# Weight sums on GpSimd, one pool, loads in program order and stage borders by tiles in a decoder trunk in split fp32

## The chip, the cores and the metric

The kernel runs on one core of one Trainium2 chip. The metric is the device time of an execution in microseconds; below it is the median of the timed runs.

## The reference

One layer of a decoder trunk on x of 1024 tokens by 1024 channels, in fp32:

```
h  = rmsnorm(x);  z = h @ W_in               # 36 column blocks of 128
yA = conformer: GLU -> causal conv of 31 taps -> LayerNorm -> silu -> @ W_a
yB = short conv: B * conv3(C * V) -> @ W_b
x1 = x + (sigmoid(gA) * yA + sigmoid(gB) * yB) @ W_o
f  = gelu(conv3(rmsnorm(x1) @ W_up gate)) * (rmsnorm(x1) @ W_up value)   # 2816 channels
x2 = x1 + f @ W_down
x3 = x2 + sigmoid(rmsnorm(x2) @ W_pg) * (p @ W_p)
out = rmsnorm(x3)
```

## The kernel before

Channels lie on the 128 partitions and the 1024 tokens along the free axis, so a 128x1024 tile holds one block of channels. Each fp32 operand is kept as a high half, which a ScalarE cast makes (`hi`), and a low half, which VectorE makes by subtracting (`lo`); a block of a product is three matmuls of 128x512, hi by hi, hi by lo and lo by hi (`halve`, `split`, `mm`). Weights arrive as fp32 and are split on the chip too: `whi` and `wlo` for a whole block of 128x1024 (names `wr_hi`, `wr_lo` for those kept).

The stages, in order:

1. The start: the embedding product, the norm, and the first four input products as whole blocks.
2. The in stage: W_in in 16 pairs of column blocks, each by a Strassen scheme of seven products (`Pair.step(m)`, m from 1 to 7) in place of eight. A product m has 12 matmuls, a pair 84. `block_order` interleaves a pair with the next. Weight operands are quarters of a pair or one of four sums of quarters (s12 and s34, in `operand`), activation operands likewise (`right_sums`). The convs of 31 taps run in the background on VectorE (`bg`, `pump`); their results go to memory in `acc_d`, the short conv's in `s_d`, the gates in `gate_d`.
3. The b stage (four steps jj of two products by `half_products`, one w_b block a step), with the LayerNorm's mean and variance formed between its steps; the a stage (the same with w_a), which ends in the merged m; the o stage (eight products by w_o), which gives x1 and the activation operands of the up stage.
4. The up stage: 22 pairs of W_up by the same scheme; f goes to `f_d`.
5. The down stage in three chunks of 8, 8 and 6 blocks of f (`DCHUNKS`), then the tail: the embedding gate's eight products by w_pg over three stretches of tokens (`SEGS`, class `Item`), the final norm and the output. The tail's ScalarE and VectorE code is in the order written.

`Loader` issues weight loads and splits. `get(ahead=2)` returns the operand of the next product after it has split those up to two whole blocks further on (three in the tail), which is how far the casts stand ahead of the products that use them. PE runs in program order; on other engines a scheduler at build time fixes an order, and each engine then takes its instructions in that order. Loads stand on SP's queue.

## Time and profile before

| | |
|---|---|
| median of 3 timed runs | 1421.42 us (1421.0 to 1421.55) |
| the profiled execution, whole | 1422.73 us |
| its span in the profile | 1420.7 us |
| TensorE, busy in the span | 94% |
| VectorE, ScalarE, GpSimd, busy | 71%, 38%, 0% |
| mean granted TensorE clock | 0.97 of full |

The profiled execution is 1.31 us longer than the median, and its span 2.03 us shorter than itself. TensorE is the engine that is busy nearly throughout, so a stage is read by where TensorE waits in it and for whom.

### The profile page before, as it was taken

Reading aid. Unit: us, or ns where it says so; the run is one execution under the profiler, and the core shown is the slowest. Engines: PE = TensorE matmul, PEld = TensorE weight load, DVE = VectorE, ACT = ScalarE, POOL = GpSimd, SP = SyncE. Lnnn points to the kernel's source line nnn. Section 1 sums busy time; section 2 is a strip of 40 time slices with the busy share of each in tenths; the row PEclk is TensorE's granted clock in tenths of the full one; section 3 lists DMA queues with packets and bytes.
Section 4 is the critical chain, followed back from the end, with each engine's and each line's share of the span. In section 5 each row is a group of like instructions: output and inputs, shape, how many; then the busy total and the mean of one; then the engine's idle time right before and its main releaser. Section 6 shows DMA issues by size and latency. Waiting matters only on the chain.

```text
span 1420.7 us, 15176 instructions
## 1 busy us (share of the span) xinstructions
PE 1336.7 (94%) x5926; PEld 1101.5 (78%) x5926; DVE 1003.8 (71%) x1290; ACT 542.7 (38%) x788; POOL 1.2 (0%) x9
## 2 busy tenths in 40 slices
PE   9799999899989599979999999999978999999996
PEld 7678687678867488868888888888856888888896
DVE  6789999999834874678777777777764332145777
ACT  7342342233441523454444344344433221023554
POOL 0000000000000000000000000000000000000000
PEclk9899999999998799989999999999998999999998
DMA  9111231122455233422222222222255431111232
GB/s 358 61 30 45 81 127 60 45 104 92 160 175 195 89 121 117 141 82 74 90 89 89 68 81 83 81 89 90 90 175 220 153 119 37 45 52 54 88 93 93
DMA packets 46727, 146.88 MB, mean 103 GB/s; under 512 B 5184, under 2 KB 11584, under 8 KB 46656
## 3 DMA queue, kind: packets, MB, share of 16 engines
q1 hardware_dynamic: 46656, 145.92, 29.4%
q8 instruction: 46, 0.75, 0.2%
q14 instruction: 25, 0.20, 0.0%
HBM read 109.20 MB, written 36.70 MB: 103 GB/s over the span
## 4 chain that ended last, share of the span: by engine, by line
PE 73%; DVE 17%; DMA 5%; ACT 3%; issue 2%; SPq 0%; DVEq 0%; ACTq 0%
PE ps L569 39%; PE ps L158 33%; DVE acc L649 7%; DVE wb L136 2%; DMA x<-xT 2%; DMA x_d<-x 1%; DVE x L875 1%; DMA f<-f_d 1%; DVE sc_cv L649 1%; DVE lrstd L328 0%; DVE s L204 0%; DMA gate<-gate_d 0%; DMA x_raw<-xT 0%; DMA p_raw<-pT 0%; DMA s<-s_d 0%
## 5 line engine op out<-in xcount | busy, mean ns | idle before, releaser
L649 DVE SCALAR_TENSOR_TENSOR acc<-a,prm,acc 128x1023 f32<-128x1023 f32 (+14 forms) x120 | 155.0, 1291 | 0.0
L135 ACT CAST wb<-s 128x512 fp32r<-128x512 f32 x152 | 90.3, 618 | 114.3 <-DVE s L213 64.6
L158 PE MATMUL ps<-f_hi,whi 128*128 128x512 f32 x352 | 109.2, 392 | 16.3 <-ACT f_hi L135 16.3
L569 PE MATMUL ps<-xgs_hi,wb 128*128 128x512 f32 x352 | 116.4, 391 | 5.2 <-ACT xgs_hi L135 5.2
L957 DVE TENSOR_TENSOR x<-ps,x 128x512 f32<-128x512 f32 x46 | 29.6, 686 | 128.8 <-PE ps L158 128.8
L135 ACT CAST whi<-raw 128x1024 fp32r<-128x1024 f32 (+2 forms) x46 | 45.7, 996 | 194.8 <-PE ps L158 175.3
L569 PE MATMUL ps<-xgt_hi,wb 128*128 128x512 f32 x352 | 116.9, 393 | 0.7 <-ACT u L595 0.7
L569 PE MATMUL ps<-xg_hi,wb 128*128 128x512 f32 x352 | 115.6, 390 | 0.0
L136 DVE TENSOR_TENSOR wb<-s,wb 128x512 fp32r<-128x512 f32 x152 | 103.6, 695 | 10.0 <-ACT wb L135 9.9
L158 PE MATMUL ps<-f_lo,whi 128*128 128x512 f32 x352 | 109.3, 392 | 0.0
L158 PE MATMUL ps<-f_hi,wlo 128*128 128x512 f32 x352 | 108.9, 391 | 0.0
L569 PE MATMUL ps<-hss_hi,wb 128*128 128x512 f32 x256 | 88.7, 408 | 12.7 <-ACT wb L135 6.2
L158 PEld LDWEIGHTS ps<-f_hi,whi 128*128 128x128 f32 x352 | 66.5, 189 | 30.3 <-ACT f_hi L135 16.7
L569 PE MATMUL ps<-h_hi,wb 128*128 128x512 f32 x256 | 85.4, 395 | 2.2 <-DVE s L596 2.2
L569 PE MATMUL ps<-hst_hi,wb 128*128 128x512 f32 x256 | 84.4, 391 | 0.9 <-ACT u L595 0.7
L136 DVE TENSOR_TENSOR wb<-raw,wb 128x512 fp32r<-128x512 f32 x114 | 79.0, 694 | 6.6 <-ACT wb L135 6.6
L569 PEld LDWEIGHTS ps<-xgs_hi,wb 128*128 128x128 f32 x352 | 66.4, 189 | 19.1 <-ACT xgs_hi L135 5.6
L569 PEld LDWEIGHTS ps<-xgt_hi,wb 128*128 128x128 f32 x352 | 66.9, 190 | 15.1 <-ACT u L595 1.1
L158 PEld LDWEIGHTS ps<-f_lo,whi 128*128 128x128 f32 x352 | 66.2, 189 | 14.7 <-DVE f_lo L136 1.1
L158 PEld LDWEIGHTS ps<-f_hi,wlo 128*128 128x128 f32 x352 | 66.4, 189 | 13.8
L569 PEld LDWEIGHTS ps<-xg_hi,wb 128*128 128x128 f32 x352 | 66.1, 188 | 13.6
L569 PEld LDWEIGHTS ps<-hss_hi,wb 128*128 128x128 f32 x256 | 48.9, 194 | 29.5 <-DVE wb L136 9.5
(226 smaller groups left out, 2850.7 us busy)
## 6 DMA issues: line engine op xcount, KB each, us to landing
raw<-w_up SPq DMA_DIRECT2D x44, 512.0 KB, 3.4
raw<-w_in SPq DMA_DIRECT2D x36, 512.0 KB, 3.6
f_d<-v_t SPq DMA_DIRECT2D x22, 512.0 KB, 3.0
f<-f_d SPq DMA_DIRECT2D x22, 512.0 KB, 6.7
gate_d<-gate SPq DMA_DIRECT2D x16, 512.0 KB, 2.7
gate<-gate_d SPq DMA_DIRECT2D x16, 512.0 KB, 5.9
raw<-w_dn SPq DMA_DIRECT2D x16, 512.0 KB, 3.6
x_raw<-xT SPq DMA_DIRECT2D x16, 256.0 KB, 6.3
```

What stands on the lines that cost most here:

```text
L135: nc.scalar.copy(hi, src)
L136: nc.vector.tensor_sub(lo, src, f32(hi))
L158: nc.tensor.matmul(ps[:, :step], wt[:, b], xt[:, t : t + step], start=f, stop=l)
L569: nc.tensor.matmul(ps, wt[:, b], xt, start=f, stop=l, skip_group_check=True)
L649: nc.vector.scalar_tensor_tensor(dst[:, s:], src[:, : T - s], w(k), dst[:, s:], ALU.mult, ALU.add)
L875: nc.vector.tensor_add(r[:, c], ps, r[:, c])
L957: nc.vector.tensor_add(x1[j][:, c], ps, x1[j][:, c])
```

## The change

The four weight sums of a pair are made by GpSimd in place, in tiles that are loaded a second time for it; a pair's loads grow from 1 MB to 2 MB. Signs are turned so that only additions are needed; some sigmoids, conv taps (`neg_b`, `neg_f`) and two of the activation sums carry the sign, and the products of a pair are taken in another order. Of a pair's weight splits, seven of 128x512, three of 128x1024 and one of 128x512 remain.

The three pools become one of 51 slots. `Loader` sorts its loads by a distance ahead, counted in matmul passes of 512 columns (`AHEAD`), and SP's queue runs in program order too. Splits have a distance of their own, `SPLIT = 40` passes, where a whole block of 128x1024 counts 6 * 8 = 48 passes.

At the borders of stages, work goes by tiles: the s tiles are loaded and split within the last steps of the in stage, the gates of the b stage ahead of it, the LayerNorm's mean and variance are formed after steps jj = 0 and jj = 1, m is split by halves, the o stage runs by halves of the tokens with its norm by halves, six f tiles are loaded and split within the last steps of the up stage, and the first four products of the down stage start on two f tiles. The w_up loads are held until the o stage is nearly over.

```diff
-NRAW, NW, NBIG = 4, 6, 41
+NBIG = 51
+AHEAD = {"whole": 100, "r": 110, "q": 100, "s": 150}
+SPLIT = 40
...
     class Loader:
...
+        def add(self, src, nb, cuts=(), again=False):
+            key = ("whole", len(self.uses))
+            n = len(self.uses)
+            self.loads.append((n, "whole", key, (src, cuts, nb)))
+            self.splits.append((n, key, (cuts, nb)))
+            self.use(key, None, 6 * nb)
...
-                st = slot("s12")
-                WADD[0](nc).tensor_add(st[:, :q], a21, a22)
-                WADD[1](nc).tensor_sub(st[:, q:], st[:, :q], a11)
...
-                st = slot("s34")
-                WADD[2](nc).tensor_sub(st[:, :q], a11, a21)
-                WADD[3](nc).tensor_sub(st[:, q:], a12, s12[:, q:])
...
+            if kind == "r":
+                t = slot("raw_r")
+                nc.sync.dma_start(t, w1)
+            elif kind == "q":
+                t = slot("raw_q")
+                nc.sync.dma_start(t[:, :q], w2[:, q:])
+            else:
+                t, v = slot("s12"), slot("s34")
+                s1, s2, s3, s4 = t[:, :q], t[:, q:], v[:, :q], v[:, q:]
+                nc.sync.dma_start(s1, w2[:, :q])
+                nc.sync.dma_start(s2, w1[:, :q])
+                nc.sync.dma_start(v, w1)
+                a22 = slot("raw_a22")
+                nc.sync.dma_start(a22[:, :q], w2[:, q:])
+                for dst, src in ((s3, s1), (s1, a22[:, :q]), (s2, s1), (s4, s2)):
+                    nc.gpsimd.tensor_add(dst, dst, src)
...
-        def get(self, ahead=2):
+        def get(self, load=True):
+            i = self.at
             self.at += 1
-            i = self.at - 1
-            n, left = i + 1, ahead * 2
-            while left > 0 and n < len(self.specs):
-                left -= 1 if self.specs[n][0] == "block" else 2
-                n += 1
-            self.split(n)
+            now = self.cost[i]
+            while load and self.loaded < len(self.loads):
+                n, kind, key, _ = self.loads[self.loaded]
+                if n > i and (key[0] in self.held or self.cost[n] - now > AHEAD[kind]):
+                    break
+                self.fetch(self.loaded + 1)
+            while self.pending and (
+                self.pending[0][0] <= i or load and self.cost[self.pending[0][0]] - now <= SPLIT
+            ):
+                self.split(*self.pending.pop(0)[1:])
...
-    with tc.manual_schedule(engines={PE}):
+    with tc.manual_schedule(engines={PE, SP}):
...
-            TADD(nc).tensor_sub(t24[:, H0], xb[:, H1], t13[:, H0])
-            TADD(nc).tensor_sub(t24[:, H1], xb[:, H0], t24[:, H0])
+            nc.vector.scalar_tensor_tensor(t24[:, H0], t13[:, H0], -1.0, b1, ALU.mult, ALU.subtract)
+            nc.vector.scalar_tensor_tensor(t24[:, H1], t24[:, H0], -1.0, b0, ALU.mult, ALU.subtract)
...
+            left = len(in_order) - 1 - n
+            for at, c in ((8, 0), (7, 1), (2, 2), (1, 3)):
+                if left == at:
+                    s_t.append(load_split(s_d[c], "s"))
...
-        s_t = [split(load(s_d[c], "s"), "s") for c in range(KC)]
...
-            if jj == 2:
-                ssq = Ssq()
+            if jj == 0:
                 pm = [bank(), bank()]
...
-        inverse(lr)
+            if jj == 1:
+                for c in HALVES:
+                    ps = bank()
+                    cs_mm(ps, ones_c, cs, c)
+                    sqrt(lr[:, c], ps)
+                    inverse(lr[:, c])
...
-                m_t[j] = split(g, "m")
+                for c in HALVES:
+                    m_t[j, c.start] = half_split(g[:, c], "m")
...
+        def o_add(i, q, c):
+            j = i + 4 * q
+            r, h = xs[i, c.start], HALVES[q]
+            if q == 0:
+                xg[i, c.start] = slot("xg")
+            nc.vector.tensor_add(r[:, h], obank[j, c.start], r[:, h])
+            nc.scalar.activation(xg[i, c.start][:, h], r[:, h], AF.Copy, scale=col("g_ffn", j))
+            nc.sync.dma_start(x1_d[j][:, c], r[:, h])
...
+            left = len(up_order) - 1 - n
+            if left in (8, 7, 2, 1):
+                for _ in range(1 if left > 2 else 2):
+                    f_t.append(load_split(f_d[len(f_t)], "f"))
...
+                    ws = [ld.get() for _ in range(4)]
+                    pss = [[bank(), bank()] for _ in range(4)]
+                    for ks in (range(2), range(2, n)):
...
-            wpg = [ld.get(2), ld.get(1)]
+            wpg = [ld.get(), ld.get()]
...
-                    wpg.append(ld.get(3))
+                    wpg.append(ld.get())
```


ScalarE at the border of the b and a stages and through the a stage. `m_hi` and `m` are casts of the merged tile `gate`, two tiles a step; a step's products use one `whi`. Before, where the four steps of the a stage use whi_3177, 3272, 3372 and 3448 in turn, and the o stage 3524, 3600 and on:

```order
L135 CAST m_hi_3431<-gate_3366 128x1024
L135 CAST whi_3448<-raw_3370 128x1024
L135 CAST m_hi_3438<-gate_3368 128x1024
L135 CAST whi_3524<-raw_3446 128x1024
L135 CAST m_hi_3507<-gate_3442 128x1024
L135 CAST m_hi_3514<-gate_3444 128x1024
L135 CAST whi_3600<-raw_3522 128x1024
L135 CAST m_hi_3583<-gate_3518 128x1024
L135 CAST m_hi_3590<-gate_3520 128x1024
L135 CAST whi_3672<-raw_3598 128x1024
L135 CAST m_hi_3659<-gate_3594 128x1024
L135 CAST m_hi_3666<-gate_3596 128x1024
```

Of the change, where the steps use whi_3356, 3432, 3508 and 3584 in turn:

```order
L130 CAST m_3415<-gate_3214 128x512
L130 CAST m_3418<-gate_3214 128x512
L130 CAST m_3424<-gate_3216 128x512
L130 CAST m_3427<-gate_3216 128x512
L130 CAST whi_3432<-raw_3292 128x1024
L130 CAST m_3491<-gate_3218 128x512
L130 CAST m_3494<-gate_3218 128x512
L130 CAST m_3500<-gate_3220 128x512
L130 CAST m_3503<-gate_3220 128x512
L130 CAST whi_3508<-raw_3354 128x1024
```

The place on PE in the changed kernel where the step on whi_3356 ends and the next begins:

```order
L153 MATMUL ps_3386<-an_lo_3211,whi_3356 128x512
L153 MATMUL ps_3387<-an_lo_3211,whi_3356 128x512
L153 MATMUL ps_3386<-an_hi_3210,wlo_3357 128x512
L153 MATMUL ps_3387<-an_hi_3210,wlo_3357 128x512
L153 MATMUL ps_3436<-an_hi_3192,whi_3432 128x512
L153 MATMUL ps_3437<-an_hi_3192,whi_3432 128x512
```

Before, the cast of the last step's whi_3448 stood right behind the first tile of the first step (gate_3366), two steps early. Now the cast of the second step's whi_3432 stands behind the second tile of the first step (gate_3216), whose product is the one just ahead of it on PE; and so at each step after.

ScalarE over the LayerNorm. `acc` holds the conv results, `cs_hi` feeds the sums over channels, the `acc<-acc` rows are the silu. Before, where the first `whi` is that of the third step of the a stage, and the last that of the fourth:

```order
L135 CAST whi<-raw 128x1024
L325 ACT_TABLE_LOAD
L325 ACTIVATE lrstd<-ps,eps_t 128x512 x2
L839 ACT_TABLE_LOAD
L839 ACTIVATE acc<-acc,prm 128x1024 x2
L135 CAST an_hi<-acc 128x1024
L839 ACTIVATE acc<-acc,prm 128x1024
L135 CAST an_hi<-acc 128x1024
L839 ACTIVATE acc<-acc,prm 128x1024
L135 CAST an_hi<-acc 128x1024 x2
L135 CAST m_hi<-gate 128x1024
L135 CAST whi<-raw 128x1024
```

Of the change, where the first single `whi` is that of the b stage's step jj = 1, and the first of the three at the end that of step jj = 2:

```order
L130 CAST cs_hi<-ssq 128x1024
L130 CAST whi<-raw 128x1024
L362 ACT_TABLE_LOAD
L362 ACTIVATE lrstd<-ps,eps_t 128x512 x2
L890 ACT_TABLE_LOAD
L890 ACTIVATE acc<-acc,prm 128x1024 x2
L130 CAST an_hi<-acc 128x1024
L890 ACTIVATE acc<-acc,prm 128x1024
L130 CAST an_hi<-acc 128x1024
L890 ACTIVATE acc<-acc,prm 128x1024
L130 CAST an_hi<-acc 128x1024 x2
L130 CAST whi<-raw 128x1024 x3
```

Before, every w_b cast, and three of w_a, stood ahead of the silu. Now the cast for b step jj = 1 stands behind the squares and the cast of their sum, and the one for jj = 2 behind the whole silu and its four casts.

ScalarE in the tail, first stretch of tokens. `last<-last` is the gate's sigmoid of a product, `x1<-x1` scales the result, `last<-x1` and `fs<-x1` are squares, `whi` the next product's weights. Before:

```order
L1014 ACTIVATE x1_7301<-x1_7301,prm_69 128x448
L1008 ACTIVATE last_8831<-x1_7303 128x448
L135 CAST whi_8951<-raw_8902 128x1024
L135 CAST whi_8957<-raw_8949 128x1024
L995 ACTIVATE last_8961<-last_8961 128x448
L1014 ACTIVATE x1_7303<-x1_7303,prm_69 128x448
L1008 ACTIVATE last_8916<-x1_7305 128x448
L135 CAST whi_8995<-raw_8955 128x1024
L995 ACTIVATE last_8999<-last_8999 128x448
L1014 ACTIVATE x1_7305<-x1_7305,prm_69 128x448
```

Of the change:

```order
L1138 ACTIVATE fs_8920<-x1_7359 128x448
L1127 ACTIVATE last_8922<-last_8922 128x448
L1146 ACTIVATE x1_7359<-x1_7359,prm_63 128x448
L1140 ACTIVATE last_8843<-x1_7361 128x448
L130 CAST whi_8957<-raw_8835 128x1024
L1127 ACTIVATE last_8961<-last_8961 128x448
L1146 ACTIVATE x1_7361<-x1_7361,prm_63 128x448
L1140 ACTIVATE last_8922<-x1_7363 128x448
L130 CAST whi_8997<-raw_8908 128x1024
```

Before, the casts for the sixth and seventh product (whi_8951, whi_8957) stood ahead of the fourth product's sigmoid (last_8961). Now the cast for the fourth product (whi_8957) stands behind the third product's sigmoid (last_8922) and the square behind it; and so for each up to the eighth.

## Rows read from the trace of the kernel before

**Rows 1.** The page, busy time of each engine (share of the span) and instructions

```profile
PE 1336.7 (94%) x5926; PEld 1101.5 (78%) x5926; DVE 1003.8 (71%) x1290; ACT 542.7 (38%) x788; POOL 1.2 (0%) x9
```

**Rows 2.** Windows: busy us (instructions) of PE, PEld, DVE, ACT, POOL; PEclk; DMA share; GB/s

```profile
140.00:320.00 180.00, 167.61 (x703) 132.00 (x702) 180.00 (x218) 56.97 (x101) 0.00 (x0) 0.98 0.24 83
400.00:440.00 40.00, 34.11 (x128) 25.48 (x127) 13.40 (x15) 12.91 (x16) 0.00 (x0) 0.87 0.71 263
460.00:500.00 40.00, 24.01 (x94) 18.47 (x92) 32.64 (x32) 19.54 (x19) 0.00 (x0) 0.79 0.21 79
488.00:494.00 6.00, 3.42 (x7) 2.31 (x8) 4.98 (x5) 6.00 (x7) 0.00 (x0) 0.50 0.00 0
620.00:660.00 40.00, 31.92 (x128) 25.01 (x127) 31.14 (x36) 19.42 (x27) 0.00 (x0) 0.87 0.20 66
636.00:642.00 6.00, 4.69 (x10) 3.41 (x11) 5.88 (x8) 3.63 (x5) 0.00 (x0) 0.50 0.00 0
700.00:1000.00 300.00, 300.00 (x1325) 248.59 (x1325) 223.39 (x315) 123.51 (x189) 0.00 (x0) 1.00 0.24 83
1040.00:1080.00 40.00, 23.03 (x92) 17.62 (x92) 21.99 (x24) 13.78 (x14) 0.00 (x0) 0.79 0.80 298
```

**Rows 3.** Waits of PE: engine and line waited for, total us, times, longest

```profile
PE ps L158 <- ACT f_hi L135: 16.3, 1, 16.3
PE ps L158 <- ACT an_hi L135: 15.2, 1, 15.2
...
PE ps L569 <- ACT xgs_hi L135: 5.2, 1, 5.2
```

**Rows 4.** The chain that ended last in order of time: start us, us, what

```profile
128.45 1.18 DVE acc L649
...
302.45 0.73 DVE wb L136
...
422.04 5.31 DMA s<-s_d
427.37 1.05 ACT s_hi L135
...
478.42 6.46 DVE lrstd L328
```

**Rows 5.** Groups of VectorE by form: xcount, busy us, mean ns, idle before

```profile
L136 DVE TENSOR_TENSOR wb<-s,wb 128x512 fp32r<-128x512 f32 x152 | 103.6, 695 | 10.0 <-ACT wb L135 9.9
...
L136 DVE TENSOR_TENSOR wlo<-raw,whi 128x1024 fp32r<-128x1024 f32 x36 | 43.8, 1219 | 13.0 <-PE ps L569 8.4 <-ACT whi L135 4.6
...
L204 DVE TENSOR_TENSOR s<-raw 128x512 f32<-128x512 f32 x38 | 26.4, 696 | 0.0
...
L850 DVE TENSOR_TENSOR gate<-ps,gate 128x512 f32<-128x512 f32 x16 | 10.3, 686 | 7.8 <-PE ps L158 5.8 <-DMA gate<-gate_d 1.9
...
L851 DVE TENSOR_TENSOR gate<-gate 128x1024 f32<-128x1024 f32 x8 | 9.8, 1222 | 0.1
...
L328 DVE RECIPROCAL rstd<-rstd 128x512 f32<-128x512 f32 x2 | 6.7, 3352 | 8.2 <-ACT rstd L325 8.2
...
L998 DVE TENSOR_TENSOR last<-last 128x448 f32<-128x448 f32 x8 | 5.0, 620 | 0.1
```

**Rows 6.** Groups of ScalarE by form, columns as above

```profile
L135 ACT CAST wb<-s 128x512 fp32r<-128x512 f32 x152 | 90.3, 618 | 114.3 <-DVE s L213 64.6 <-DVE s L204 38.2 <-PE ps L569 5.3
...
L135 ACT CAST whi<-raw 128x1024 fp32r<-128x1024 f32 x36 | 37.8, 1051 | 138.1 <-PE ps L158 130.8 <-PE ps L569 7.3
...
L839 ACT ACTIVATE acc<-acc,prm 128x1024 f32<-128x1024 f32 x4 | 4.9, 1237 | 9.3 <-DVE acc L838 9.3
...
L995 ACT ACTIVATE last<-last 128x448 f32<-128x448 f32 x8 | 4.6, 580 | 10.3 <-DVE last L992 10.3
```

**Rows 7.** The only 128x512 instruction of GpSimd, by form

```profile
L309 POOL MEMSET warm<- 128x512 f32 x1 | 0.5, 528 | 0.0
```

**Rows 8.** DMA issues: KB each, median us from issue to landing

```profile
acc<-acc_d SPq DMA_DIRECT2D x4, 512.0 KB, 10.2
```

More of the change, by code (lines that the diff above doesn't have):

```diff
@@ new lines, in split @@
+        def split(self, key, arg):
+            t = self.raw.pop(key)
+            if key[-1] == "q":
+                w = slot("w_q", F32R)
+                hi, lo = w[:, :DC], w[:, DC:]
+                halve(hi, lo, t[:, :DC])
+            elif key[0] == "whole":
+                cuts, nb = arg
+                hi, lo = slot("whi", F32R), slot("wlo", F32R)
+                edges = [0, *cuts, nb]
+                for a, b in zip(edges, edges[1:]):
+                    c = slice(a * P, b * P)
+                    halve(hi[:, c], lo[:, c], t[:, c])
+            else:
+                hi, lo = split(t, "w_" + key[-1])
+            self.done[key] = (hi, lo)
@@ L290, in trunk_kernel @@
         ld.add(w_o[j], 8)
[L291 removed]
+    ld.add_pairs("up", [(w_up[KF + j], w_up[j]) for j in range(KF)], up_order)
     f0 = 0
@@ L882, in trunk_kernel, with load_x1, o_mm @@
-        cs = cs_split(ssq.acc)
-        rstd = slot("rstd1")
+                for c in HALVES:
+                    m_t[j, c.start] = half_split(g[:, c], "m")
+        rows = [{} for _ in range(4)]
+        ws, obank, xs, xg, osum = {}, {}, {}, {}, {}
+        def load_x1(i, c):
+            r = slot("x1")
+            for q, j in zip(HALVES, (i, 4 + i)):
+                nc.sync.dma_start(r[:, q], xT[j * P : (j + 1) * P, c])
+            xs[i, c.start] = r
+        def o_mm(j, c, ks, first, last):
+            if j not in ws:
+                ws[j] = ld.get()
+            if first:
+                obank[j, c.start] = bank()
+            ps = obank[j, c.start]
+            whi, wlo = ws[j]
+            for k in ks:
+                b = slice(k * P, (k + 1) * P)
+                hi, lo = m_t[k, c.start]
+                nc.tensor.matmul(ps, whi[:, b], hi, start=first and k == ks[0], stop=False)
+                nc.tensor.matmul(ps, whi[:, b], lo, start=False, stop=False)
+                nc.tensor.matmul(ps, wlo[:, b], hi, start=False, stop=last and k == ks[-1])
@@ new lines, in o_plain, with o_sums, o_rstd @@
+        def o_plain(i):
+            hi, lo = split(xg[i, 0], "xgp")
+            rows[i][1], rows[i][2] = (hi[:, H0], lo[:, H0]), (hi[:, H1], lo[:, H1])
+        def o_sums(i):
+            x0, x1 = xg[i, 0], xg[i, HB]
+            rows[i].update(sum_halves(*right_sums(x0[:, H0], x1[:, H0], x0[:, H1], x1[:, H1]), "xg"))
+            rows[i][3] = half_split(x1[:, H1], "xgq")
+        rstd = slot("rstd1")
+        def o_rstd(c, cs):
+            ps = bank()
+            for i, q in enumerate(HALVES):
+                for x, y in ((0, i == 0), (1, False)):
+                    nc.tensor.matmul(ps, ones_d, cs[x][:, q], start=y, stop=x == 1 and i == 1)
+            sqrt(rstd[:, c], ps)
+            inverse(rstd[:, c])
@@ L942, in trunk_kernel @@
         for ci, n in enumerate(DCHUNKS):
-            f_t = [split(load(f_d[f0 + k], "f"), "f") for k in range(n)]
             last = ci == len(DCHUNKS) - 1
```

427 lines of the change are left out of this document (217 added, 210 removed).

## The prediction

> **What bounds it now.** I read the page's busy times first: TensorE is busy for 94% of the span, VectorE for 71%, GpSimd for nothing [rows 1]. TensorE is therefore the bound, and the question is where it falls short. The windows answer it by counting matmuls. In the up stage it runs 1325 of them in 300 us at full clock [rows 2], which is 0.2264 us each, or 4.417 a microsecond. The same count elsewhere gives what a stretch loses, waits and slow clock together: 140 to 320 us holds 703 where 795 would fit, so 20.8 us; 400 to 440 holds 128 of 176.7, 11.0 us; 460 to 500 holds 94, 18.7 us; 620 to 660 holds 128, 11.0 us; 1040 to 1080 holds 92, 19.2 us [rows 2]. That is 80.7 us in all.
>
> The waits and the chain name the causes. In 140 to 320 VectorE is busy for all 180 us [rows 2], and from 128.45 to 302.45 us the chain runs on its taps (L649) and splits [rows 4]. At 400 to 440 TensorE waits for an s tile's load (5.31 us) and cast [rows 4]; at 460 to 500 for an_hi, 15.2 us, behind a reciprocal of 6.46 us [rows 3, 4]; at 620 to 660 for xgs_hi, 5.2 us; at 1040 to 1080 for f_hi, 16.3 us [rows 3]. After such a wait the clock is low: PEclk is 0.50, the lower of the two levels, at 488 to 494 and 636 to 642 us, and ten matmuls keep TensorE 4.69 us there against 2.26 at full clock [rows 2]. I charge 2 us for each wait of about 5 us or more.
>
> **The gains, part by part.**
>
> *Sums and splits, in stage.* Four sums of 0.696 us leave VectorE per pair, 2.78 us. Seven splits of 0.695 become three of 1.219 and one of 0.695, 0.51 us less [rows 5]. That is 3.3 us a pair; 140 to 320 us holds 703/84 = 8.4 pairs, so 27.6 us of relief against 20.8 lost. VectorE stops being the bound, and the most that can come back is 20.8. The adds on GpSimd have no row: its only 128x512 operation is a memset of 0.528 us [rows 7], and the longest row of that size on any engine is a reciprocal, 3.352 us [rows 5]. Four a pair then take 2.1 to 13.4 us, under the 84 x 0.2264 = 19.0 us that TensorE needs, so GpSimd is no bound. What they do to VectorE is a rival below. I take -15, between 0 and -20.8. In the up stage VectorE is busy for 223 of 300 us with no wait of TensorE [rows 2]; the same relief is worth nothing there. The second load of weights adds 38 MB, and the DMA share there is 0.24 [rows 2]; doubled, it still hides.
>
> *Borders.* Loading s within the in stage takes away most of the 11.0 us at 400 to 440: -9. The LayerNorm wait of 460 to 500 goes from its place: -18.7 (it returns below). The o to up loss goes from its place: -11.0 (also returns). Six f tiles ahead take all but 3 us of 1040 to 1080: -16. Sum of gains: -15 - 9 - 18.7 - 11 - 16 = -69.7.
>
> **The losses.** A whole weight block counts 48 passes and SPLIT is 40, so no full block is split before the product that uses it is asked for. ScalarE takes its rows in order, and the order shows the cast of the next whi behind casts that need the product just ahead. TensorE has nothing else to do meanwhile. The same pattern explains the waits of before: an_hi, xgs_hi and f_hi are each the cast right behind which TensorE's next product stands [rows 3].
>
> *b stage, jj = 1.* Behind the mean: eight subtractions of 128x512 from a bank (nearest row 0.686), two additions of 1.222 among them, then a square and a cast at 1.05 each, the last addition 1.222, and whi 1.05 [rows 5, 6]: 12.3 us, less some overlap, 11.5, plus 2 of clock: 13.5.
>
> *b stage, jj = 2.* Before, the variance to the first an_hi took the 15.2 us wait [rows 3]. Now the cast stands behind the whole silu: two more silu of 1.237 and three more casts of 1.05, and whi itself 1.05, 6.7 us on top [rows 6], less some 2 us because the reciprocal starts by halves: 20, plus 2: 22.
>
> *a stage, three steps, and the first o product.* After the last matmul: two gate multiplications at 0.686, an addition 1.222, two casts of a half at 0.618, whi 1.051 [rows 5, 6]: 4.9 us, plus 2, four times: 27.6.
>
> *o stage and up's start.* The product that follows the first four waits for two evictions, the sums, xgs, xgt, xgq and then whi, worked out from the same rows as 8 + 2. Three later ones wait for an addition 0.686, a copy 0.62, whi 1.05, one of them for a square too: 2.4 + 3.4 + 2.4. The norm's cs_lo: 1.9. The first up product needs the last x1, then a reciprocal 3.352, four sums, four casts, a square and its own w_r_hi, 13 + 2. Together 35.1 us.
>
> *Tail.* For products four to eight: multiplication 0.612 to 0.62, sigmoid 0.58, two or three VectorE operations of 0.62, a square as long as the sigmoid, whi 1.051, and wlo (1.219) which only two matmuls cover [rows 5, 6]: 4.9 us, five times, and 2 for the third: 26.5. Work between these waits is short (24 matmuls, some 5 us), so the clock may stay low: 0 to 20 us, I take 8.
>
> *Start.* The first pair's w_r_hi now stands behind casts of the fourth input product: +1.
>
> Losses: 13.5 + 22 + 27.6 + 35.1 + 26.5 + 8 + 1 = 133.7. Net +64.0. The profiled execution, 1422.7 us, would become 1486.7; it stands 1.3 us above the median, so the median goes to about 1485.
>
> **Rivals.**
>
> *GpSimd blocks VectorE (0.17).* Most VectorE operations of the in stage read two tiles of SBUF, as GpSimd's adds do. If each add held VectorE up by 0.82 us, the relief of 3.3 us a pair would be gone; the bounds for an add, 0.528 and 3.352 us, lie on both sides of that [rows 5, 7]. With 1.4 us each (twice the 0.696 of the same addition on VectorE), a pair costs VectorE 2.3 us more than before, over 8.4 pairs +19 in place of -15: about 1519. Nothing in the trace before bears on it, since GpSimd does nothing there after the start. In the up stage VectorE has 76 us of 300 free, 4.8 us a pair before the relief, and would still hide it.
>
> The Trainium skill ("SBUF — State Buffer", "Who interferes with whom") says that a VectorE instruction with two SBUF inputs contends with a GpSimd instruction that reads SBUF, the later of the two blocking until the first is done. By its measured ratio for this addition ("GPSIMD Engine Reference"), 1.96 times VectorE's time, an add would be an estimated 1.36 us, and by that rule taken in full the in stage would lose about what the rival above says. No run before shows it.
>
> *Loads late at the b stage (0.10).* SP's queue issues eight gates and then four acc tiles, 6 MB, after the last gate store of the in stage. At 298 GB/s, what the busiest of my windows moved [rows 2], that is 21 us, while the first b step's products last 48 x 0.2264 = 10.9 us. An acc tile took 10.2 us to land before [rows 8]. Then jj = 1 waits some 10 us longer: about 1495.
>
> *The waits hardly show (0.08): faster.* If what stands ahead of each cast were done before the product ends, because evictions of its first half run early, each of the 18 waits that I count would cost only its own cast and half a wlo, some 1.9 us: 34 in place of 133.7, so about 1386. The point from which it decides: the waits must come to less than 69.7 us together, 3.9 each on average. Against it: both halves of a product end within one matmul of each other, and an_hi cost its full 15.2 us before [rows 3].
>
> *The clock stays low (0.05).* If the waits in the a and o stages and the tail come so close that TensorE stays at the lower level between them, a step of 48 matmuls costs 10 us more; four steps less the 8 us charged for them, and the tail's 20 in place of 8, give about 1530.
>
> **How the numbers follow.** The forecast has 0.60, with a range of its own of 1460 to 1512, from the in stage's 0 to -20.8, the tail's clock and some 10% on the chains. It is the likeliest case and gives the time, 1485. The range for all cases is 1440 to 1525: it takes in the contention and the late loads, and leaves out the faster rival, most of the low clock and the edges. This kernel's time can be told from no change to about 0.2%, 3 us. Faster 0.09, from the third rival and a little of the forecast's lower edge; the same 0.03; slower 0.88.
>
> **What would show it.** In the new trace, waits of PE for whi casts: about 5 us three times in the a stage, once at the o stage's start and five times in the tail; 11 to 20 us twice in the b stage; 13 us at the first w_r_hi. The f_hi wait of 16.3 us and the s load's wait should be gone or under 4 us. In 140 to 320 us VectorE should be below 97% busy and TensorE above 750 matmuls; if VectorE is still full and its rows are longer, GpSimd blocks it. The prediction is wrong if waits for whi stay under 4 us each, or if the b stage's chain has been overlapped with its products.

## The result and the profile after

The changed kernel takes 1579.84 us (median of 4 runs, 1574.97 to 1582.45) where the kernel before took 1421.21 (4 runs, 1420.33 to 1421.55): a ratio of 1.1113, with an interval of 1.1085 to 1.1142. It is slower, as forecast, but by 159 us where 64 were predicted, and above the range's upper end of 1525. The profiled execution has a span of 1577.0 us (before 1420.7).

First the page of the changed kernel, its busy times, the answer to [rows 1]:

```profile
PE 1381.5 (88%) x5930; PEld 1128.9 (72%) x5930; DVE 1013.7 (64%) x1036; ACT 528.9 (34%) x691; POOL 283.5 (18%) x161
```

TensorE runs four matmuls more than before and is busy for a smaller share of the span. Those matmuls took 45 us more, at a mean granted clock of 0.936 in place of 0.970. VectorE has 254 instructions fewer and is busy for 10 us more, so each of them is longer. GpSimd has 283.5 us of work.

Next the windows of the changed kernel, with the columns of [rows 2]. They stand at the same places in the program, not at the same microseconds: in stage, start of the b stage, start of the down stage, tail.

```profile
140.00:320.00 180.00, 159.74 (x656) 126.90 (x656) 178.41 (x147) 49.09 (x67) 57.33 (x30) 0.95 0.36 120
440.00:480.00 40.00, 22.73 (x91) 17.62 (x90) 18.57 (x23) 13.15 (x14) 0.00 (x0) 0.80 0.92 348
...
1160.00:1200.00 40.00, 19.41 (x68) 15.11 (x68) 20.26 (x19) 15.34 (x15) 0.00 (x0) 0.70 0.84 325
1432.00:1510.00 78.00, 52.07 (x175) 42.18 (x174) 29.55 (x36) 20.59 (x32) 0.00 (x0) 0.78 0.09 25
```

In the in stage 180 us now hold 656 matmuls, 47 fewer than before, and VectorE is still full (178.41 of 180) with 147 instructions in place of 218. That is the sign that the prediction named for a GpSimd that blocks VectorE; the longer rows that go with it stand under e2.

The waits of PE in the changed kernel, with the columns of [rows 3]:

```profile
PE ps L153 <- ACT whi L130: 98.8, 15, 17.6
PE ps L604 <- DVE w_r_lo L131: 23.9, 10, 4.6
PE ps L927 <- ACT whi L130: 22.9, 5, 10.0
PE ps L604 <- ACT w_r_hi L130: 15.2, 2, 12.0
```

The waits for an_hi, xgs_hi and f_hi are gone. In their place stand 22 waits for the cast of a weight, 136.9 us; only one of them, 8.0 us at the start, has a counterpart before (7.9 us, for wr_hi). Single ones of them, from the timeline of PE in the changed kernel (start, duration, instruction, and in brackets the idle time before it and who ended it):

```profile
476.88 0.80 PE L153 MATMUL ps<-s_hi,whi 128*128 128x512 f32 x1 [16.06 <-ACT whi L130]
508.56 0.80 PE L153 MATMUL ps<-s_hi,whi 128*128 128x512 f32 x1 [17.57 <-ACT whi L130]
...
656.20 0.80 PE L927 MATMUL ps<-m,whi 128*128 128x512 f32 x1 [10.01 <-ACT whi L130]
735.44 0.79 PE L604 MATMUL ps<-xgp_hi,w_r_hi 128*128 128x512 f32 x1 [12.01 <-ACT w_r_hi L130]
1180.13 1.22 PE L153 MATMUL ps<-f_hi,whi 128*128 128x512 f32 x2 [14.94 <-ACT whi L130]
...
1467.62 0.74 PE L153 MATMUL ps<-xp_hi,whi 128*128 128x448 f32 x1 [3.99 <-ACT whi L130]
```

To book the 156.3 us of span by stage, take where the products of the stages meet on PE, in the changed kernel: the first with s, the first with an, the last of the up stage, the first of the tail.

```profile
447.95 0.62 PE L153 MATMUL ps<-s_hi,whi 128*128 128x512 f32 x2
531.97 0.62 PE L153 MATMUL ps<-an_hi,whi 128*128 128x512 f32 x2
1162.08 0.39 PE L604 MATMUL ps<-xgq,w_s_lo 128*128 128x512 f32 x1
1427.98 0.44 PE L153 MATMUL ps<-xp_hi,whi 128*128 128x448 f32 x1 [1.25 <-ACT sq L393]
```

The kernel before, read in the same way, has 418.56, 490.55, 1055.74 and 1315.24. The differences give the table (us; the tail ends with the span):

| stretch | before | after | difference | predicted |
|---|---|---|---|---|
| start and in stage | 418.6 | 448.0 | +29.4 | -15 + 1 = -14 |
| b stage and LayerNorm | 72.0 | 84.0 | +12.0 | -9 - 18.7 + 13.5 + 22 = +7.8 |
| a, o and up stages | 565.2 | 630.1 | +64.9 | -11 + 27.6 + 35.1 = +51.7 |
| down stage | 259.5 | 265.9 | +6.4 | -16 |
| tail | 105.5 | 149.0 | +43.5 | +34.5 |
| sum | 1420.7 | 1577.0 | +156.3 | +64.0 |

The miss of 92 us has two large parts: 43 in the in stage and 22 at the down border. The tail lost 9 more than booked, the a, o and up stages 13.

### The profile page after: what moved, and what is told of

The parts are those of the page before. It is cut to its first block, busy times and chain, and to the rows that moved or that the text cites. A ratio compares the mean times of both kernels' runs of the same rounds, so it can differ in the third digit from the quotient of the medians.

```text
span 1577.0 us, 15432 instructions
## 1 busy us (share of the span) xinstructions
PE 1381.5 (88%) x5930; PEld 1128.9 (72%) x5930; DVE 1013.7 (64%) x1036; ACT 528.9 (34%) x691; POOL 283.5 (18%) x161
## 4 chain that ended last, share of the span: by engine, by line
PE 65%; DVE 19%; DMA 4%; issue 4%; ACT 3%; SPq 0%; DVEq 0%; ACTq 0%
PE ps L604 33%; PE ps L153 26%; DVE acc L679 7%; PE ps L929 2%; PE ps L927 2%; PE ps L928 2%; DVE w_s_lo L131 2%; DVE w_r_lo L131 1%; DVE wlo L131 1%; ACT whi L130 1%; DMA raw<-w_dn 1%; DMA acc<-acc_d 1%; DVE sc_cv L679 1%; DVE lrstd L365 0%; DMA x<-x_d 0%
## 5 line engine op out<-in xcount | busy, mean ns | idle before, releaser
L228 POOL TENSOR_TENSOR s<-s,s 128x512 f32<-128x512 f32 x76 | 134.6, 1772 | 812.2 <-DVE xgq L131 327.5
L131 DVE TENSOR_TENSOR w_s_lo<-s,w_s_hi 128x1024 fp32r<-128x1024 f32 x76 | 117.1, 1542 | 10.7 <-issue 6.3
L679 DVE SCALAR_TENSOR_TENSOR fg<-u_t,neg_f,fg 128x1023 f32<-128x1023 f32 (+1 forms) x44 | 74.7, 1697 | 28.6 <-ACT fg L673 27.8
L153 PE MATMUL ps<-xp_hi,whi 128*128 128x448 f32 (+2 forms) x192 | 67.8, 353 | 24.1 <-ACT whi L130 22.8
L130 ACT CAST w_s_hi<-s 128x1024 fp32r<-128x1024 f32 x76 | 79.7, 1050 | 14.9 <-DVE a L634 7.6
L604 PE MATMUL ps<-xgp_hi,w_r_hi 128*128 128x512 f32 x176 | 70.0, 398 | 12.0 <-ACT w_r_hi L130 12.0
L228 POOL TENSOR_TENSOR s<-s 128x512 f32<-128x512 f32 x38 | 76.2, 2005 | 3.0
L927 PE MATMUL ps<-m,whi 128*128 128x512 f32 x128 | 54.7, 427 | 22.9 <-ACT whi L130 22.9
L228 POOL TENSOR_TENSOR s<-s,raw_a 128x512 f32<-128x512 f32 x38 | 71.6, 1883 | 14.2 <-PE ps L604 5.8
L130 ACT CAST whi<-raw 128x1024 fp32r<-128x1024 f32 (+2 forms) x55 | 54.2, 996 | 51.2 <-PE ps L153 34.5
L604 PE MATMUL ps<-xgp_hi,w_r_lo 128*128 128x512 f32 x176 | 69.8, 397 | 1.3 <-DVE w_r_lo L131 1.3
L604 PE MATMUL ps<-xgp_lo,w_r_hi 128*128 128x512 f32 x176 | 69.7, 396 | 0.0
```

Source lines behind the costliest of these rows:

```text
L130: nc.scalar.copy(hi, src)
L131: nc.vector.tensor_sub(lo, src, f32(hi))
L153: nc.tensor.matmul(ps[:, :step], wt[:, b], xt[:, t : t + step], start=f, stop=l)
L228: nc.gpsimd.tensor_add(dst, dst, src)
L604: nc.tensor.matmul(ps, wt[:, b], xt, start=f, stop=l, skip_group_check=True)
L679: nc.vector.scalar_tensor_tensor(dst[:, s:], src[:, : T - s], w(k), dst[:, s:], ALU.mult, ALU.add)
```

## The experiments

Theory: the losses are the weight casts that stand on ScalarE behind the work of the product ahead, because whole blocks count 48 against a SPLIT of 40; GpSimd's sums slow VectorE in the in stage; and the down border waits for loads that stand on SP's queue behind the last f store. The rivals differ in each.

### e1_split48: whole blocks may be split 48 passes ahead

```diff
-                self.pending[0][0] <= i or load and self.cost[self.pending[0][0]] - now <= SPLIT
+                self.pending[0][0] <= i or load and self.cost[self.pending[0][0]] - now <= (48 if self.pending[0][1][0] == "whole" else SPLIT)
```

> The changed kernel with one number changed: whole weight blocks may be split 48 passes ahead instead of 40, so each is split one product earlier. Theory A (the casts of whi stand behind work that needs the product just ahead): the waits of PE for whi, 121.7 us in the changed kernel, fall below 25 us (the first down weights and the start remain), most of the low clock after them goes too, and the time falls by 105 to 130 us, to 1450 to 1475 us. Rival B (TensorE would have waited for something else there anyway, evictions, LayerNorm or loads): the waits change their names and the time falls by less than 40 us.

1479.08 us (1471.99 to 1483.31), ratio 1.0399 (1.0357 to 1.0440): 101 us of the 159 come from this one number. The waits of PE in this kernel:

```profile
PE ps L153 <- ACT whi L130: 41.4, 5, 14.7
...
PE ps L153 <- DVE wlo L131: 12.8, 4, 9.2
...
PE ps L927 <- ACT whi L130: 4.6, 1, 4.6
```

Of 20 waits for whi (121.7 us) 6 are left (46.0). Two of them, 14.7 and 7.0, are the down border's. The 9.2 stands in the b stage behind subtractions that wait for the acc tiles' loads. The gain fell just short of the range expected, with 46 us of waits left where under 25 were expected. Booked by the marks of the table above, e1 gives back 17 us in the b stage, 49 in the a, o and up stages and 39 in the tail, which is 110.0 us long there; the in stage is 4 us later.

### e2_sums_dve and e3_no_sums: GpSimd's sums put on VectorE, and left out

The first moves the four additions of a pair back to VectorE. The second leaves the additions out altogether and keeps their loads, so its weights are not those of the reference.

```diff
-                    nc.gpsimd.tensor_add(dst, dst, src)
+                    nc.vector.tensor_add(dst, dst, src)
```

> The changed kernel with the four weight sums on VectorE instead of GpSimd, from the same tiles loaded twice, nothing else. Theory A (GpSimd's adds hold VectorE up in the in stage): VectorE's taps return from 1.48 us to about 1.29, its 128x1024 low halves from 1.54 to 1.22, and the in stage, which ends 29 us later than in the kernel before, gets 20 to 35 us back although VectorE does 2.8 us more a pair: 1545 to 1560 us. Rival B (the in stage is late because weights are loaded twice, or because SP issues in program order): VectorE has more to do and the time stays or grows, 1575 to 1620 us. In the up stage neither expects a difference.

> The changed kernel with the four weight sums of each pair left out altogether (the operands are the loaded quarters), with all the loads. Theory A (contention with GpSimd): the in stage loses both the adds and their hold on VectorE, VectorE is no longer full there and the stage ends 40 to 50 us earlier than in the changed kernel: 1527 to 1540 us. Rival B (loads late in the in stage): the loads are as before, and less than 15 us come back.

With the sums on VectorE: 1565.64 us (1563.85 to 1567.81), 14 us faster than the changed kernel. Without them: 1530.29 (one run), 50 faster. The same 280 us of the in stage (120 to 400) by windows, first in the kernel before and then in the changed kernel:

```profile
120.00:400.00 280.00, 267.61 (x1143) 214.66 (x1142) 268.32 (x328) 98.58 (x172) 0.00 (x0) 0.99 0.26 89
120.00:400.00 280.00, 253.25 (x1049) 202.16 (x1048) 277.69 (x226) 81.20 (x114) 95.69 (x50) 0.96 0.37 121
```

then with the sums on VectorE:

```profile
120.00:400.00 280.00, 257.49 (x1090) 207.08 (x1089) 268.04 (x283) 87.31 (x121) 0.00 (x0) 0.98 0.39 128
```

and without sums:

```profile
120.00:400.00 280.00, 277.11 (x1220) 228.60 (x1219) 244.05 (x241) 101.72 (x140) 0.00 (x0) 1.00 0.44 145
```

Against the changed kernel VectorE has 57 instructions more when it makes the sums itself, is busy for 10 us less, and TensorE gets through 41 matmuls more. The taps of the convolution on VectorE in the changed kernel (count, busy us, mean ns):

```profile
L679 DVE SCALAR_TENSOR_TENSOR acc<-a,prm,acc 128x1023 f32<-128x1023 f32 (+14 forms) x120 | 177.5, 1479 | 1.3
L131 DVE TENSOR_TENSOR w_s_lo<-s,w_s_hi 128x1024 fp32r<-128x1024 f32 x76 | 117.1, 1542 | 10.7 <-issue 6.3 <-ACT w_s_hi L130 4.3
```

and with the sums on VectorE:

```profile
L679 DVE SCALAR_TENSOR_TENSOR acc<-a,prm,acc 128x1023 f32<-128x1023 f32 (+14 forms) x120 | 152.1, 1267 | 1.0
L131 DVE TENSOR_TENSOR w_s_lo<-s,w_s_hi 128x1024 fp32r<-128x1024 f32 x76 | 92.7, 1221 | 10.3 <-ACT w_s_hi L130 10.3
```

The same instructions are on the mean 17% and 26% longer where GpSimd adds. That the sums come late from GpSimd is no rival: all waits for them in the changed kernel come to 2.8 us. The relief of VectorE, without the price, is what the run without sums shows: its first s product starts at 400.8 us, 18 before the kernel before. So the relief predicted was there; the adds cost more than it.

Moving the sums gave less than the 20 to 35 expected. With them on VectorE the in stage still ends 18 us later than before (first s product at 436.9), though VectorE is then as busy as before. The timeline and the waits of PE in e2 name where this rest stands:

```profile
95.14 0.79 PE L604 MATMUL ps<-h_q,w_r_hi 128*128 128x512 f32 x1 [7.43 <-ACT w_r_hi L130]
...
PE ps L604 <- DVE w_q L131: 19.3, 12, 3.8
```

Its first pair starts at 95.1 us, 8 later than before (87.0). Behind that, TensorE waits twelve times for the low half of a w_q, between 135 and 396 us, 19.3 us in all; the kernel before has waits of 11.2 us for its weight halves wb there. Why w_q is late with VectorE no busier than before (the order of a pair's products, the larger pieces, the distance of the splits) was not tried.

### e10_before_pool: the kernel before, its four sums on GpSimd

```diff
-WADD = (_vector, _vector, _vector, _vector)
+WADD = (_pool, _pool, _pool, _pool)
```

> The kernel before with one part of the change alone: its four weight sums a pair on GpSimd (38 pairs, two of the four as subtractions), single loads, all else as before. Theory A (the adds hold up VectorE more than the 2.8 us a pair that leave it): VectorE's taps grow from 1.29 to some 1.45 us or more as in the changed kernel, VectorE stays full in the in stage, and the time is 5 to 20 us above before, 1426 to 1441 us. Rival B (in the changed kernel it was the double loads and the order that made the in stage late, GpSimd's adds being nearly free): 5 to 20 us below before, 1401 to 1416 us.

1448.01 us (1445.62 to 1449.89), ratio 1.0194 (1.0179 to 1.0209): 28 us slower, above what was expected. Nothing else of the change is in this kernel, so the contention stands alone. The loss is in the in stage: the first s product starts at 443.0 us, 24 later than before, while the up stage still holds 1325 matmuls from 700 to 1000 us. Its window:

```profile
120.00:400.00 280.00, 254.14 (x1055) 201.69 (x1054) 276.77 (x266) 86.58 (x155) 99.33 (x50) 0.96 0.24 81
```

and a group of GpSimd's additions and one of VectorE's splits, by form:

```profile
L204 POOL TENSOR_TENSOR s<-raw 128x512 f32<-128x512 f32 x38 | 60.5, 1593 | 732.0 <-PE ps L158 232.4 <-DMA raw<-w_up 160.6 <-DMA raw<-w_in 129.9
...
L136 DVE TENSOR_TENSOR wb<-s,wb 128x512 fp32r<-128x512 f32 x152 | 125.1, 836 | 25.6 <-ACT wb L135 25.3
```

The splits took 695 ns before [rows 5] and take 836 here; the taps (L649) went from a mean of 1291 ns to 1414. In the same window the kernel before has 1143 matmuls: 88 more, which at 0.2264 us each are 20 us. VectorE has 62 instructions fewer here, 266 against 328, and is busy for 8 us more.

### e4_wdn_early and e5_border: the down border

The first issues the loads of the first four w_dn blocks earlier and puts the eight x1 loads behind the first down products. The second has this and the 48 of e1, and loads and splits the last two f tiles behind the four weights. The lines are e5's; e4 has those on `left` and on `x1` alone.

```diff
             left = len(up_order) - 1 - n
+            if left == 7:
+                ld.fetch(ld.loaded + 3)
             if left in (8, 7, 2, 1):
...
-        while len(f_t) < DCHUNKS[0]:
-            f_t.append(load_split(f_d[len(f_t)], "f"))
-        x1 = [load(x1_d[j], "x1") for j in range(KD)]
...
                     ws = [ld.get() for _ in range(4)]
+                    while len(f_t) < DCHUNKS[0]:
+                        f_t.append(load_split(f_d[len(f_t)], "f"))
...
+                    x1 = [load(x1_d[i], "x1") for i in range(KD)]
```

> The changed kernel with the loads of the first four w_dn blocks issued ahead of the last steps of the up stage, and the eight x1 loads behind the first down products instead of ahead. Theory A (the waits of 14.9 and 5.7 us for whi at the start of the down stage are w_dn loads that stand on SP's queue behind the store of the last f tile and the x1 loads): both go, except for some 2 us, and with the slow clock after them 17 to 23 us come back: 1557 to 1563 us. Rival B (the wait is for the last f result and its cast, as in the kernel before): the wait turns into one for f_hi of 10 to 15 us and less than 8 us come back.

> On top of whole blocks split 48 passes ahead (1479 us): four w_dn blocks loaded ahead of the last up steps, the last two f tiles of the first chunk loaded and split behind the weights of the first four down products, x1 loads behind those. Theory A (the 14.7 us wait at the start of the down stage is not the w_dn load but ScalarE's order: the cast of the second w_dn block stands behind the casts of the last two f tiles, whose loads stand on SP's queue behind the store of the last f): with that order undone the waits of 14.7 and 7.0 us both go but for 3 us, and with their slow clock 18 to 24 us come back: 1455 to 1461 us. Rival B (the last up result itself, its conv and gelu, is what is late on ScalarE): the first wait stays above 8 us and less than 12 us come back.

e4: 1575.09 us (1574.04 to 1576.98), only 5 faster at the medians, with ranges that overlap, where 17 to 23 were expected. The second wait of the border, 5.65 us, is gone; the first, 14.94, is still 13.26. The chain in order of time shows why. In the changed kernel it goes from the load of w_dn, 10.18 us from 1179.38, to the cast behind the second wait, and that is the one that e4 removes. The cast behind the first wait stands on ScalarE at 1179.04 us, right behind the casts of the last two f tiles (1176.22 and 1178.08). In e4:

```profile
1177.49 0.32 SPq L1043
...
1178.34 5.52 DMA f<-f_d
...
1183.88 1.05 ACT f_hi L130
1184.93 0.96 ACT whi L130
```

The weight is there, but its cast stands on ScalarE behind the casts of the last f tiles, and their loads stand on SP's queue behind the last f store (L1043). e5: 1464.52 (1463.54 to 1466.04), ratio 1.0306 (1.0290 to 1.0321), 14.6 faster than e1, where 18 to 24 were expected; the first wait of the down stage is now 5.47 us and the second is gone. The down stage itself gained 18 us, but the last up steps before it became 4 us longer, in e4 5: a wait of 1.94 us for w_s_lo is new there, and the granted clock behind it is low (0.83 from 1149.5 to 1169.8 us in e4). So the border is a queue in program order, on SP and on ScalarE both; e4 alone opens only one of them.

### e6_in_dve: 48, and the in stage's sums alone on VectorE

```diff
-                    nc.gpsimd.tensor_add(dst, dst, src)
+                    (nc.vector if key[0] == "in" else nc.gpsimd).tensor_add(dst, dst, src)
```

> On top of whole blocks split 48 passes ahead (1479 us): the sums of the in stage on VectorE, those of the up stage still on GpSimd. Theory A (GpSimd's adds cost something only where VectorE is full): the same 13 to 16 us come back as with all sums on VectorE, 1463 to 1466 us, and the up stage is as long as with GpSimd, within 2 us. Rival B (contention costs TensorE time in the up stage too): the gain is below 8 us, the rest being in the up stage.

1460.12 us (1458.93 to 1464.56), ratio 1.0282 (1.0258 to 1.0305), 19 faster than e1, above the 13 to 16 expected. The up stage, where GpSimd still adds, in this kernel by windows:

```profile
700.00:1000.00 300.00, 300.00 (x1325) 248.43 (x1324) 223.36 (x207) 119.72 (x143) 119.88 (x64) 1.00 0.40 137
```

It holds the same 1325 matmuls in 300 us as before [rows 2], beside 120 us of GpSimd's additions: there VectorE has room for the longer instructions. e10 showed the same. The contention costs time in the in stage, where VectorE is full, and none in the up stage, where it is not.

### e7_all: all of these, and loads moved forward

The sums as in e6, the border as in e5, whole blocks split right behind the issue of their loads (100 passes ahead, like the loads, in place of 48), the acc loads ahead of the gates', and the first two up weights fetched and split within the o stage.

```diff
+        acc = [load(acc_d[c], "acc") for c in range(KC)]
         gs = load_gates(KD)
-        acc = [load(acc_d[c], "acc") for c in range(KC)]
...
                     ld.held.clear()
+                    ld.fetch(ld.loaded + 3)
+                    ld.split_to(ld.at + 2)
```

> The changed kernel with whole blocks split 100 passes ahead, sums of the in stage on VectorE, the border of the down stage as in the run before last, the acc tiles loaded ahead of the b stage's gates, and the first two weights of the up stage loaded and split inside the o stage. Theory A (the loss is the sum of these five places): from 1580 us, -105 for the casts, -14 for the sums, -20 for the down border, -10 to -16 for the b stage, -6 to -12 for the first up weights: 1413 to 1425 us, level with the kernel before. Rival B (removing one wait uncovers another at the same place): 1440 us or more.

1430.12 us (1426.45 to 1431.13), ratio 1.0058 (1.0040 to 1.0077): 150 us of the 159 are back, 5 us short of the range expected, and it is not faster than before. The in stage is still late as in e2 (first s product at 438.0 us). The other waits went elsewhere, by the waits of PE and the timeline of ScalarE in this kernel:

```profile
PE ps L604 <- DVE w_q L131: 18.3, 11, 3.8
PE ps L967 <- ACT cs_hi L130: 12.0, 2, 11.5
...
PE ps L382 <- ACT cs_hi L130: 7.2, 1, 7.2
...
460.28 1.05 ACT L130 CAST whi<-raw 128x1024 fp32r<-128x1024 f32 x1 [17.70 <-DMA raw<-w_b]
...
626.70 1.04 ACT L130 CAST w_r_hi<-raw_r 128x1024 fp32r<-128x1024 f32 x1 [3.66 <-DMA raw_r<-w_up]
```

Splitting weights earlier puts their casts ahead of the norms' squares and cs_hi, and there a cast waits for its own load: 17.70 us for a w_b in the b stage, until 626.70 us for the second up weight in the o stage. What stands behind it waits too: the squares, whose last inputs are done at 457.4 and 622.6 us, start at 461.2 and 627.7. The waits of TensorE for cs_hi, 7.2 and 11.5 us, are in part these. What is scarce is a place in ScalarE's order, not its time: it was busy for 34% of the changed kernel's span.

### e11_before_noahead: the kernel before, without splitting whole blocks ahead

```diff
-            while left > 0 and n < len(self.specs):
+            while left > 0 and n < len(self.specs) and self.specs[n][0] == "block":
```

> The kernel before with whole weight blocks split only when their own product asks for them, as the changed kernel's 40 passes have it; single quarters as before. Theory A (the distance alone makes the casts late): the waits for whi of the changed kernel appear in the b, a and o stages and in the tail, 80 to 105 us: 1500 to 1525 us. Rival B (with buffers of their own for split weights, the scheduler takes these casts early wherever it is free to, and the distance decides only where ScalarE's order is written out, in the tail): waits for wr_hi and whi in the tail alone, 4 us for each of six products and its slow clock: 1445 to 1465 us.

1465.45 us (1464.94 to 1466.76), ratio 1.0319 (1.0304 to 1.0334). The waits of PE in this kernel:

```profile
PE ps L158 <- ACT wr_hi L135: 25.1, 5, 8.1
...
PE ps L158 <- ACT whi L135: 12.0, 3, 4.0
```

All of these but one at the start, of 7.9, which the kernel before has too, stand in the tail, and the later ones there are 3.45 to 3.99 us, as in the changed kernel; the loss of 45 us is near the tail's 43.5 in the table above. In the b, a and o stages there is no wait for a weight: without a split ahead the casts still stood in front of the product's work there. In the changed kernel they did not: by e1 that is where the 101 us came from that the tail did not give. Split weights have buffers of their own before and share one pool after; whether that is the reason was not tried.

### e8, e9 and e12: the borders alone, on the kernel before

e8 takes from the change only the early loads of s tiles and of six f tiles. e9 adds that x1 is loaded behind the first chunk's f tiles. e12 adds the LayerNorm one step earlier: its means at the first b step, its squares at the second, its reciprocal and silu ahead of the fourth step's product.

```diff
+            if left in (8, 7, 2, 1):
+                for _ in range(1 if left > 2 else 2):
+                    f_e.append(split(load(f_d[len(f_e)], "f"), "f"))
...
+            if ci == 0:
+                x1 = [load(x1_d[j], "x1") for j in range(KD)]
...
-            if jj == 1:
+            if jj == 0:
                 pump(len(bg))
...
-            if jj == 2:
+            if jj == 1:
                 ssq = Ssq()
```

> The kernel before with one part of the change alone: the s tiles loaded and split within the last steps of the in stage and six f tiles within the last steps of the up stage; weights, sums, order of SP and everything else as before. Theory A (those two border gains were real and the changed kernel lost them to its order of casts and loads): the wait for s, 5.3 us and its neighbours, and most of the 16.3 us wait for f_hi go, 18 to 27 us come back: 1394 to 1403 us. Rival B (the waits at the borders are for the last results of the stage before, so that an early load moves nothing): less than 6 us come back.

> The kernel before with the two border parts of the run before last (1416.6 us) and one more: the eight x1 loads at the start of the down stage issued behind the first chunk's f loads instead of ahead of them. Theory A (the 13.95 us wait for f_hi that was left there is the last two f loads standing on SP's queue behind 4 MB of x1): it falls to 4 us or less, and with the slow clock 10 to 14 us come back: 1402 to 1407 us, below both kernels. Rival B (the last f's store and its way through memory take that long by themselves): less than 5 us come back.

> The run that beat both (the kernel before with its two borders by tiles and x1 behind f, 1406.5 us) and one more part of the change: the LayerNorm's mean and variance one step earlier, the variance and silu ahead of the fourth b step's products on PE. The weight casts still stand ahead of the silu there. Theory A (the early LayerNorm is a gain by itself, which the changed kernel lost to the casts behind it): the 13.7 us wait for an_hi falls to 5 us or less, 8 to 13 us come back: 1393 to 1399 us. Rival B (the acc tiles land too late for it): a wait of some 8 us or more for cs_hi takes its place, and less than 5 us come back.

e8: 1416.6 us (10 runs, 1415.04 to 1419.81), ratio 0.9971 (0.9962 to 0.9981): 5 us, where 18 to 27 were expected. The f_hi wait is still 13.9, and SP's queue in the timeline of this kernel shows what stands in front of the last f tiles:

```profile
1059.25 4.86 SPq L778 DMA_DIRECT2D x<-x_d  x8
1065.04 4.15 SPq L778 DMA_DIRECT2D f<-f_d  x4
```

The eight x tiles are the loads of x1. e9: 1406.51 (1405.24 to 1408.26), ratio 0.9907 (0.9890 to 0.9923), 10 us faster than e8, f_hi down to 3.5 and 3.0. e12: 1399.19 (1398.41 to 1402.35) against 1420.29, ratio 0.9852 (0.9831 to 0.9872), 7 us faster than e9 and the fastest of all. Its waits of PE:

```profile
PE ps L158 <- ACT f_hi L135: 6.6, 2, 3.5
...
PE ps L158 <- ACT an_hi L135: 5.3, 1, 5.3
```

The two waits of 16.3 and 15.2 us [rows 3] have become 6.6 and 5.3. So the border part of the change is worth its gain when it comes without the rest; in the change the rest took it back.

## Why the prediction was off

The direction and the main mechanism hold. "No full block is split before the product that uses it is asked for" is borne out by e1 (101 us from that number alone), and the single waits came out near their sums: a stage 4.53 to 4.59 against 4.9, o stage 10.01 against 8, then 2.47, 3.42 and 2.47 against 2.4, 3.4 and 2.4, up 12.01 against 13, tail 3.99 against 4.9, b at jj = 2 17.57 against 20. At jj = 1 it was 16.06 against 11.5. There the rival of late loads was partly right: on the changed kernel's chain the gates' load (5.71 us) and an acc tile's (10.17, as [rows 8] have it) stand ahead of the mean's subtractions; in e1, where the cast of whi stands earlier, TensorE still waits 9.2 us there behind the same two loads.

```profile
450.11 5.71 DMA gate<-gate_d
...
455.88 10.17 DMA acc<-acc_d
```

**The step that failed: "Sums and splits, in stage ... I take -15, between 0 and -20.8".** The stretch lost 29 us. The relief was sized rightly: from the start of the first pair to the first s product it takes 331.6 us before and 311.5 without the sums (e3), 20 less. What failed is the term for GpSimd's adds, put at nothing: with them it takes 354.4, 43 more than without them, where the same sums on VectorE (341.8) cost 30. So of the 29 us 6.5 stand at the start, 13 are what the adds cost more on GpSimd than on VectorE, and 10 are left with the sums on VectorE, where TensorE waits for w_q; these last were in no term. The bounds left a loss out, though the rival held it. Nothing in the trace before bore on it, and I took the side on which the row said least. The rival (GpSimd blocks VectorE, 0.17) had the mechanism. Its terms: an add was to hold VectorE up by 0.82 us or more, the adds to take 0.528 to 3.352 us. In the changed kernel they take 1772 to 2005 ns, by GpSimd's groups (count, busy us, mean ns):

```profile
L228 POOL TENSOR_TENSOR s<-s,s 128x512 f32<-128x512 f32 x76 | 134.6, 1772 | 812.2 <-DVE xgq L131 327.5 <-DMA s<-w_up 164.0 <-DMA s<-w_in 137.1
L228 POOL TENSOR_TENSOR s<-s 128x512 f32<-128x512 f32 x38 | 76.2, 2005 | 3.0
```

The rival's +19 in place of -15 is near the 22.9 that the stage lost behind its start and the 24 of e10's, but its time of 1519 was still 61 us short, for the terms below. That VectorE is the in stage's bound [rows 2] was read rightly; what was missing is that moved work can make the work that stays longer.

The Trainium skill ("SBUF — State Buffer", "Who interferes with whom") says that a VectorE instruction with two SBUF inputs contends with a GpSimd instruction that reads SBUF. The runs agree with it: such instructions of VectorE get longer while GpSimd adds, and in e2 and e3 they do not; those that take one input from a PSUM bank (L634, v_t<-ps,u) have a mean of 678 ns in the changed kernel and 691 in e2. The estimate of 1.36 us for an add, from the ratio in the Trainium skill's "GPSIMD Engine Reference" (3.1, "Elementwise — side-by-side cycle accounting"), is near what an add takes with nothing on VectorE beside it, 1.29 us at 743.56 us; beside VectorE's work the adds took 1.8 to 2.0.

**The second: "Six f tiles ahead take all but 3 us of 1040 to 1080: -16".** The down stage lost 6 us. The last two of eight f tiles, x1 and w_dn are issued on SP behind the last f store, and the whi cast stands behind the f_hi casts; the waits of 14.94 and 5.65 took the place of the 16.3. I followed the tiles and not the queue that they stand in; e4, e5, e8 and e9 show both queues.

**Sizes.** The tail lost 43.5 where 26.5 + 8 were booked. Its waits were smaller than charged (seven, of 1.68 to 3.99 us, 22.8 in all, and five of half a microsecond for wlo), so the larger part of the rest is put down to the clock, 0.78 in 1432 to 1510 us, where I charged 8 us. No run takes the one away without the other; e1 takes both, and its tail runs at a granted clock of 1.00 in 1371 to 1449 us. The a and o stages lost some 13 more than booked, for the same reason or for one not told apart. The term for the start, +1, was 6.5: the first w_r_hi wait there is 3.2 us, and the first pair's product starts at 93.5 in place of 87.0.

Of the rivals "hardly show" and "clock stays low" the first is excluded by the waits (the longest 17.57), the second came near its price in the tail (43.5 less 22.8 and 2.8 leaves 18, of its 20), and is not seen at its price in the a and o stages.

## What to carry to other kernels

Before you give work from a full VectorE to an idle GpSimd, try it by itself: here the instructions that stayed became 17 to 26% longer, and the stage became longer where it was to become shorter, while a stage with a quarter of VectorE free did not notice. When loads or casts are moved to an earlier place, write down each in-order queue that they pass (SP's behind a store, ScalarE's behind evictions) and see that both are open; one alone gives nearly nothing. A cast that is put ahead of the arrival of its own load holds up all that stands behind it, as in e7. A threshold that decides what is prepared ahead must be checked against the largest piece: 40 against 48 was worth 101 us.

## What was not expected of the hardware

Instructions of both engines are longer while both run, and they are so by turns. From the timelines of VectorE and GpSimd in the changed kernel, around 234 us, and one add with nothing on VectorE beside it:

```profile
233.28 1.21 DVE L131 TENSOR_TENSOR w_s_lo<-s,w_s_hi 128x1024 fp32r<-128x1024 f32 x1
233.41 2.24 POOL L228 TENSOR_TENSOR s<-s,raw_a 128x512 f32<-128x512 f32 x1 [1.11 <-DVE acc L679]
234.41 2.29 DVE L679 SCALAR_TENSOR_TENSOR acc<-a,prm,acc 128x1002 f32<-128x1002 f32 x1
235.72 2.12 POOL L228 TENSOR_TENSOR s<-s 128x512 f32<-128x512 f32 x1
...
743.56 1.29 POOL L228 TENSOR_TENSOR s<-s,raw_a 128x512 f32<-128x512 f32 x1
```

The low half w_s_lo, which started first, keeps its 1.21 us and ends at 234.49. The add that started behind it ends at 235.65, 1.16 us after that. The tap that started behind the add ends at 236.70, 1.05 us after the add, and the next add at 237.84, 1.14 us after the tap. So here each instruction finishes some 1.1 us after the one of the other engine that was running when it started; for 1.24 of the tap's 2.29 us the add was still running. That agrees with the Trainium skill ("SBUF — State Buffer", "Who interferes with whom"), by which the later of the two waits until the first is done. A tap and an add by turns take 2.2 us, less than the 1.27 and 1.29 us that they take alone; by the ends, 0.1 to 0.2 us of each pass while the other still runs.
